# Cached keys rearranged in DRAM ahead of the attention stage, bias rows of the samples built once, and the T sums on VectorE

## The chip, the cores and the metric

The kernel runs on one core of one Trainium2 chip. A core has five engines with an instruction queue each: TensorE (PE in the profile, its weight loads PEld), VectorE (DVE), ScalarE (ACT), GpSimd (POOL) and SyncE (SP). An engine works through its queue in order; an instruction that waits for a semaphore holds up all that is queued behind it. SyncE computes nothing here: its queue only issues transfers, and GpSimd and ScalarE issue some too. All transfers of the core share 16 DMA engines. The metric is the device time of one execution in microseconds (us).

## The reference

One step of an encoder trunk for two groups with the same weights: 512 new rows of one stream (the prompt) and 16 new rows for each of 8 running streams (the samples), 640 rows of 2048 values in all. A shared projection w_in makes queries, keys, values and gates for 16 heads: 6 stick-breaking heads, 6 chunk-band softmax heads with a learned bias by distance, and 4 heads into memory tokens. The samples also attend to cached keys and values.

```python
(sq, sk, sv, sg, bq, bk, bv, bg, mq, mg, gsb, gbd, gmm) = in_projection(x, g_pre, w_in)
k_all = concatenate([cache_sb_k, sk2], axis=1)              # 8 x (512 + 16) x 6 x 128
o_sb2 = stick_breaking(sq2, k_all, v_all, q_pos_s, k_pos_sb)
o_bd2 = band_attention(bq2, kb, vb, q_pos_s, k_pos_bd, rel_bias)   # softmax(q k^T / sqrt(128) + bias)
o_mm2 = memory_attention(mq2, cache_mem_k, cache_mem_v)     # 8 x 256 x 4 x 128
merged = sigmoid(gsb)*((o_sb*silu(sg)) @ w_up_sb) + sigmoid(gbd)*(...) + sigmoid(gmm)*(...)
y = x + rms_norm(merged @ w_out, g_post)
```

Everything is float32. The keys, values and outputs of the new rows are returned as well.

## The kernel before, in words

**Precision.** Each float32 operand is split into a high part (ScalarE copies and rounds) and a low part (VectorE subtracts); the helper `split` does both, at L101 and L102, for every operand in the program. A product is three matmuls: high by high, high by low, low by high. So each 128x512 piece of weight costs one ScalarE and one VectorE instruction before TensorE can use it.

**Stages.** First the memory tokens are projected and the normed rows are transposed into x (tiles xh, xl, in four quarters b11, b12, b21, b22). Then four *gates*: column blocks of w_in, each 96 matmuls at L173. Beside them `sums` (L690 to L701) makes the operands T1 to T4 of a Strassen-type scheme out of the quarters of x: for each of four pieces k it adds high and low part of the four quarters (L695, tiles r1, r2, r3, r4; b11 and b12 on VectorE, b22 and b21 on GpSimd), stores r3, which is b12 again, to DRAM (L696), subtracts four times (L698, three on GpSimd and the last on VectorE) and splits the results (tiles th, tl). The tiles rs are taken from the three buffers of the tag ws.

**The pair stage.** 34 *pairs* of 128-column blocks of w_in follow (`block_pair`): `load_quads` (L716) loads four tiles of 512 KB on SP's queue, GpSimd forms the sums and differences s1 to s4 of weight quarters (L730, L777; the same tag ws), and TensorE does seven products of 24 matmuls each (L737). The first 12 pairs make the queries, keys, values and gates of the band heads, which go to DRAM (raw_d); the others make merge gates (sig_d). The weight tiles have three buffers in each of two tags (wr and wr2), so loads run about a pair ahead, each waiting until the split of an earlier tile has released its buffer.

**The attention stage.** 16 heads in a fixed order by a list of numbers. For each head the remaining projections run (L173, weights by L128), and three generators are interleaved: the prompt's attention, the samples' scores and the samples' outputs. For the scores `sample_score` brings in the cached keys of two streams at a time: `load_k` (L495) issues four transfers, one for each 32 columns of the head, which take runs of 32 values (128 bytes) and set them in the tile kc so that a blockwise transpose of VectorE (L506, tile kt) gives keys by columns. kc has two buffers. The cached values come by L546 (tile vc, eight transfers a head). For a band head the bias rows of the samples are loaded in eight transfers of 16 partitions (L594, tile st1) and eight of 16x8x16 values (L598, st3); GpSimd masks st3 twice and reorders it to st2 (L603, L605). natk (L629) is a store: new keys go out in four transfers of 128-byte runs.

**The end.** The up-projections follow (L173 again, results merged at L861 to L864), then the output projection (L158 to L160) and the norm.

The program is written with a tile framework. A scheduler that simulates a timeline sets the final order of every engine's queue, so instructions of neighbouring heads and pairs are mixed; `issue_after(x)` makes an instruction stand behind x in that order. These are the lines for the keys and for T:

```python
SP.dma_start(t[32 * a:32 * a + 32],                       # L495, for a in 0..3
             ck[b:b + 2, :, 32 * a:32 * a + 32].rearrange("b (c j) i -> j (b c) i", j=32))
DVE.transpose(kt, kc[:, h * nc_:(h + 1) * nc_])           # L506
for eng, t, q in ((DVE, r1, b11), (POOL, r2, b22), (DVE, r3, b12), (POOL, r4, b21)): ...      # L695
for eng, t, x, y in ((POOL, r1, r3, r1), (POOL, r3, r2, r3), (POOL, r2, r2, r1), (DVE, r4, r4, r2)): ...  # L698
```

Of the kernel before, what the change touches and what calls it, by code (L numbers as in the profile page):

```python
# [8 lines left out]
F32 = mybir.dt.float32  # L9
F32R = mybir.dt.float32r  # L10
AF = mybir.ActivationFunctionType
ALU = mybir.AluOpType
# [4 lines left out]
P = 128  # L17
# [4 lines left out]
NB = 8  # L22
TS = 16
NT = TP + NB * TS
HF = NT // 2
PAST = 512
NMEM = 256
# [11 lines left out]

C_SB, C_BD, C_MM, C_GATE = 0, 3072, 6144, 7168  # L40
# [3 lines left out]
def stream_step_kernel(  # L44
# [29 lines left out]


# [5 lines left out]
    kv_d = dpool.tile([NMEM, 1024], F32, name="kv_d")  # L81
    osg_d = [dpool.tile([P, NT], F32, name=f"osg_d{i}") for i in range(16)]
# [4 lines left out]
    sig_d = [dpool.tile([P, NT], F32, name=f"sig_d{i}") for i in range(3 * KB)]  # L87

# [105 lines left out]
    with ExitStack() as m0:  # L194
# [45 lines left out]
        mtmp = pm.tile([P, P], F32, name="mtmp")  # L240
# [7 lines left out]
        POOL.tensor_scalar(nsb, msb, -1.0, 1.0, op0=ALU.mult, op1=ALU.add)  # L248

# [29 lines left out]
        def load_bias():  # L279
# [4 lines left out]
            POOL.dma_start(rext_d, rext)  # L284

# [48 lines left out]

    def ext_ap(h, off, dims):
        t = rext_d[h:h + 1, off:off + 1]
        return bass.AP(tensor=t.tensor, offset=t.offset, ap=dims)
# [147 lines left out]
    def sample_score(ck, qr, kr, kind, strips, left):  # L485

        nkb = ck.shape[1] // P
        nc_ = nkb * P
        new = kind != "mm"

        def load_k(b):

            t = pa.tile([P, 32, 32], F32, tag="kc", name="kc", bufs=B["kc"])[:, :2 * nc_ // 32]
            for a in range(4):
                SP.dma_start(t[32 * a:32 * a + 32],  # L495
                             ck[b:b + 2, :, 32 * a:32 * a + 32].rearrange("b (c j) i -> j (b c) i", j=32))
            return t.rearrange("p c i -> p (c i)")
# [85 lines left out]
    def causal_head(i):  # L583

        kind, h, c0 = ("sb", i, C_SB) if i < 6 else ("bd", i - 6, C_BD)
        ck, cv = ((cache_sb_k, cache_sb_v), (cache_band_k, cache_band_v))[i // 6]
        kp, vp, ks, vs = (tokens(t)[:, h] for t in ((sbk_p, sbv_p, sbk_s, sbv_s), (bdk_p, bdv_p, bdk_s, bdv_s))[i // 6])
        strip, strips = None, None
        if kind == "bd":
            strip = pa.tile([P, 512], F32, tag="strip", name="strip")  # L590
            SP.dma_start(strip, ext_ap(h, 0, [[1, P], [1, 512]]))
            st1 = pa.tile([P, 512], F32, tag="st1", name="st1")
            for bb in range(NB):
                SP.dma_start(st1[bb * TS:(bb + 1) * TS], ext_ap(h, 128, [[1, TS], [1, 512]]))  # L594
            st2 = pa.tile([P, P], F32, tag="st2", name="st2")
            st3 = pa.tile([P, P], F32, tag="st3", name="st3")
            for bb in range(NB):
                SP.dma_start(st3[bb * TS:(bb + 1) * TS], ext_ap(h, 112, [[1, TS], [0, NB], [1, TS]]))  # L598

            with tc.issue_after(last_on(POOL)):  # L600
                POOL.memset(strip[0:64, 0:64], NEG)
                for base, cm, step in ((TS - P, 1, TS), (P - 1, -1, -TS)):
                    POOL.affine_select(st3, st3, pattern=[[step, NB], [0, TS]], compare_op=ALU.is_ge,  # L603
                                       fill=NEG, base=base, channel_multiplier=cm)
# [373 lines left out]
```

## Time and profile before

| what | value |
|---|---|
| time, median of 3 runs | 2138.67 us (2134.91 to 2139.42) |
| the profiled execution, its time | 2134.09 us |
| its span in the trace | 2132.4 us |
| PE, PEld, DVE, ACT, POOL busy in the span | 97%, 91%, 53%, 38%, 28% |
| DMA queue of SP | 541310 packets, 265.51 MB, 46.4% of 16 engines' span |
| packets under 512 bytes | 277841 of 554394 |
| chain of waits by engine | PE 85%, issue 4%, DMA 4%, DVE 2%, POOL 2%, SP's queue 2% |

A busy share is a mean over stages. The stages follow each other in time: memory and norm until 78 us, gates until about 134, pairs until 981, attention until about 1733, then up-projection and output. PE's busy time hides one thing: the granted clock, which falls to half for some microseconds after TensorE has stood still, is a column of its own. "Waits" name for each idle time of an engine what ended it; the chain goes back from the last instruction through what released each step.

### The profile page before, as it was taken

How to read it: one execution, taken by the hardware profiler on the slowest of the kernel's cores; microseconds unless marked ns; L12 is line 12 of the kernel's file. 1: busy time of each engine (PE TensorE's matmuls, PEld its weight loads, DVE VectorE, ACT ScalarE, POOL GpSimd, SP SyncE). 2: the span in 40 equal slices, each digit the busy share in tenths (PEclk: the TensorE clock that was granted, in tenths of full speed). 3: DMA queues.
4: the chain of work that ended last, by engine and by line, in shares of the span. 5: the costliest groups of instructions: out<-in, count | busy, mean ns of one | idle time of the engine just before them, and what ended most of it. 6: DMA issues, size and time to landing. Idle time of an engine off the chain costs nothing.

```text
span 2132.4 us, 36113 instructions
## 1 busy us (share of the span) xinstructions
PE 2058.5 (97%) x13997; PEld 1945.9 (91%) x13997; DVE 1128.3 (53%) x1788; ACT 815.5 (38%) x1567; POOL 599.0 (28%) x557
## 2 busy tenths in 40 slices
PE   8999999999999999999998899999997899999998
PEld 6999999999999999999988798989996799998886
DVE  6895555565555555554445546554445554542234
ACT  7534444444444444443223334333333232332221
POOL 0385455664444444440010101110100004330000
PEclk9999999999999999999999999999999899999999
DMA  7633333333333333335858669875665966542225
GB/s 248 198 105 115 129 121 105 105 104 115 123 127 104 105 104 112 124 122 119 196 125 206 143 152 201 208 157 137 151 160 134 249 182 193 173 133 79 79 76 221
DMA packets 554394, 305.86 MB, mean 143 GB/s; under 512 B 277841, under 2 KB 513377, under 8 KB 552685
## 3 DMA queue, kind: packets, MB, share of 16 engines
q1 hardware_dynamic: 541310, 265.51, 46.4%
q0 software_dynamic: 6000, 22.30, 2.8%
q10 hardware_dynamic: 6912, 15.73, 1.9%
q8 instruction: 110, 1.80, 0.4%
q14 instruction: 62, 0.51, 0.1%
HBM read 258.11 MB, written 45.37 MB: 142 GB/s over the span
## 4 chain that ended last, share of the span: by engine, by line
PE 85%; issue 4%; DMA 4%; DVE 2%; POOL 2%; SPq 2%; ACT 1%; DVEq 0%; POOLq 0%; ACTq 0%
PE q L737 39%; PE acc L173 26%; PE ya L160 3%; PE ya L158 3%; PE ya L159 3%; PE s L510 1%; POOL merged L864 1%; PE o L569 1%; SPq L495 1%; DMA kc<-in_cache_sb_k_dram 1%; PE tp L438 1%; PE acc L158 1%; PE acc L160 1%; DVE wl L102 1%; PE acc L159 1%
## 5 line engine op out<-in xcount | busy, mean ns | idle before, releaser
L102 DVE TENSOR_TENSOR wl<-wr,wh 128x512 fp32r<-128x512 f32 (+1 forms) x524 | 396.4, 761 | 395.1 <-ACT wh L101 385.7
L101 ACT CAST wh<-wr 128x512 fp32r<-128x512 f32 (+1 forms) x524 | 316.4, 608 | 651.5 <-PE acc L173 250.7
L102 DVE TENSOR_TENSOR wl<-ws,wh 128x512 fp32r<-128x512 f32 x272 | 244.1, 900 | 221.4 <-ACT wh L101 220.1
L737 PE MATMUL q<-xh,wl 128*128 128x320 f32 x1088 | 338.1, 311 | 4.2 <-DVE wl L102 4.2
L737 PE MATMUL q<-xh,wh 128*128 128x320 f32 x1088 | 337.7, 310 | 0.0
L737 PE MATMUL q<-xl,wh 128*128 128x320 f32 x1088 | 337.6, 310 | 0.0
L101 ACT CAST wh<-ws 128x512 fp32r<-128x512 f32 x272 | 169.1, 622 | 270.5 <-PE q L737 231.4
L173 PE MATMUL acc<-xh,wl 128*128 128x320 f32 x1152 | 271.5, 313 | 0.0
L173 PE MATMUL acc<-xh,wh 128*128 128x320 f32 x1152 | 269.2, 313 | 0.0
L173 PE MATMUL acc<-xl,wh 128*128 128x320 f32 x1152 | 269.1, 312 | 0.0
L737 PE MATMUL q<-th,wl 128*128 128x320 f32 x816 | 252.2, 309 | 0.0
L737 PE MATMUL q<-th,wh 128*128 128x320 f32 x816 | 252.1, 309 | 0.0
L737 PE MATMUL q<-tl,wh 128*128 128x320 f32 x816 | 252.1, 309 | 0.0
L737 PEld LDWEIGHTS q<-xh,wl 128*128 128x128 f32 x1088 | 206.0, 189 | 4.8 <-DVE wl L102 4.8
L737 PEld LDWEIGHTS q<-xh,wh 128*128 128x128 f32 x1088 | 205.8, 189 | 0.1
L737 PEld LDWEIGHTS q<-xl,wh 128*128 128x128 f32 x1088 | 205.8, 189 | 0.0
L173 PEld LDWEIGHTS acc<-xh,wh 128*128 128x128 f32 x1152 | 194.4, 189 | 10.4 <-issue 7.5
L173 PEld LDWEIGHTS acc<-xl,wh 128*128 128x128 f32 x1152 | 194.9, 190 | 6.3 <-issue 6.3
L173 PEld LDWEIGHTS acc<-xh,wl 128*128 128x128 f32 x1152 | 195.2, 190 | 2.8 <-issue 2.3
L730 POOL TENSOR_TENSOR ws<-wr 128x512 f32<-128x512 f32 x102 | 148.6, 1470 | 80.0 <-DVE wl L102 78.0
L777 POOL TENSOR_TENSOR ws<-wr,ws 128x512 f32<-128x512 f32 x68 | 89.7, 1319 | 232.9 <-DVE wl L102 232.9
L737 PEld LDWEIGHTS q<-th,wl 128*128 128x128 f32 x816 | 153.2, 188 | 0.2 <-DVE wl L102 0.2
(237 smaller groups left out, 3362.6 us busy)
## 6 DMA issues: line engine op xcount, KB each, us to landing
wr<-in_w_in_dram SPq DMA_DIRECT2D x208, 512.0 KB, 4.7
wr<-in_w_out_dram SPq DMA_DIRECT2D x32, 512.0 KB, 3.8
sig_d<-sig ACTq DMA_DIRECT2D x48, 320.0 KB, 4.3
sig<-sig_d SPq DMA_DIRECT2D x48, 320.0 KB, 3.6
kc<-in_cache_sb_k_dram SPq DMA_DIRECT2D x96, 128.0 KB, 3.6
vc<-in_cache_sb_v_dram SPq DMA_DIRECT2D x48, 256.0 KB, 5.8
kc<-in_cache_band_k_dram SPq DMA_DIRECT2D x96, 128.0 KB, 3.7
vc<-in_cache_band_v_dram SPq DMA_DIRECT2D x48, 256.0 KB, 5.4
```

Of the source, the lines that this page charges most:

```text
L101: ACT.copy(hi, src)
L102: DVE.tensor_tensor(lo, src, hi.bitcast(F32), op=ALU.subtract)
L158: PE.matmul(out, ah, bh, start=start, stop=False)
L159: PE.matmul(out, ah, bl, start=False, stop=False)
L160: PE.matmul(out, al, bh, start=False, stop=stop)
L173: PE.matmul(acc[:, s, :HF], a[:, k], b[s], start=first and f, stop=last and l)
L438: PE.transpose(tp[:, kb * P:(kb + 1) * P], b[:, kb * P:(kb + 1) * P], ident)
L495: SP.dma_start(t[32 * a:32 * a + 32], ck[b:b + 2, :, 32 * a:32 * a + 32].rearrange("b (c j) i -> j (b c) i", j=32))
L510: return PE.matmul(s[32 * j:32 * j + 32, :nc_], qm[:, j, par * 32:par * 32 + 32], kts[j], start=par == 0, stop=par == 1, tile_position=(0, ...
L730: eng.tensor_tensor(o, a[c], b[c], op=op)
L737: PE.matmul(bank_, a[:, k], b[:, k], start=first and k == 0 and n == 0, stop=k == KH - 1 and n == 2, skip_group_check=not first)
L777: POOL.tensor_tensor(b, a, b, op=ALU.subtract)
```

## The change

1. `cut_keys` (new) copies the cached keys of every head from the input to new DRAM tensors keys_d, DRAM to DRAM, in the layout that kc wants. It uses the same four transfers for two streams as `load_k` did, on SP's queue. 64 such cuts of four transfers (12 heads at 128 KB a transfer, 4 memory heads at 64 KB) are handed out two after each pair from the second one on, in the heads' order (the list ORDER), behind the last SP instruction of that pair.
2. `load_k` becomes one transfer for two streams: 128 partitions of two runs of 2048 bytes (1024 for memory heads) from keys_d.
3. The bias rows of the samples are built once, after rext_d, by six DRAM to DRAM transfers of GpSimd into st_d (128 rows of 528 values for each band head). A band head then takes one load instead of sixteen. The mask (tile mbd) is made once at the start; a head's st2 is one GpSimd addition.
4. In `sums` GpSimd keeps only r4 = b21; VectorE does the other three sums and all four differences.

```diff
+ORDER = (0, 6, 1, 7, 12, 2, 8, 3, 9, 13, 4, 5, 14, 15, 10, 11)
+
 C_SB, C_BD, C_MM, C_GATE = 0, 3072, 6144, 7168
 
 
...
+    mbd = const.tile([P, P], F32, name="mbd")
+
 
     xq = [[None, None], [None, None]]
     for i, j in ((0, 0), (0, 1), (1, 0), (1, 1)):
...
+    st_d = [dpool.tile([P, TS + 512], F32, name=f"st_d{h}") for h in range(6)]
+
+    keys_d = [dpool.tile([P, NB, (NMEM if i >= 12 else PAST)], F32, name=f"keys_d{i}") for i in range(16)]
     osg_d = [dpool.tile([P, NT], F32, name=f"osg_d{i}") for i in range(16)]
...
+    def ext_ap(h, off, dims):
+        t = rext_d[h:h + 1, off:off + 1]
+        return bass.AP(tensor=t.tensor, offset=t.offset, ap=dims)
 
...
-        mtmp = pm.tile([P, P], F32, name="mtmp")
+        mtmp = pm.tile([P, P], F32, tag="junk", name="mtmp")
...
+        ntmp = pm.tile([P, P], F32, tag="junk", name="ntmp")
+        POOL.memset(ntmp, 0.0)
+        for base, cm, step in ((TS - P, 1, TS), (P - 1, -1, -TS)):
+            POOL.affine_select(ntmp, ntmp, pattern=[[step, NB], [0, TS]], compare_op=ALU.is_ge,
+                               fill=NEG, base=base, channel_multiplier=cm)
+        POOL.tensor_copy(mbd.rearrange("p (a j i) -> p a j i", a=2, i=TS),
+                         ntmp.rearrange("p (j a i) -> p a j i", a=2, i=TS))
...
             POOL.dma_start(rext_d, rext)
+
+            for h in range(6):
+                POOL.dma_start(st_d[h].rearrange("(b t) n -> b t n", t=TS),
+                               ext_ap(h, 112, [[0, NB], [1, TS], [1, TS + 512]]))
...
-        nkb = ck.shape[1] // P
-        nc_ = nkb * P
+        nc_ = ck.shape[2]
         new = kind != "mm"
 
         def load_k(b):
 
             t = pa.tile([P, 32, 32], F32, tag="kc", name="kc", bufs=B["kc"])[:, :2 * nc_ // 32]
-            for a in range(4):
-                SP.dma_start(t[32 * a:32 * a + 32],
-                             ck[b:b + 2, :, 32 * a:32 * a + 32].rearrange("b (c j) i -> j (b c) i", j=32))
-            return t.rearrange("p c i -> p (c i)")
+            t = t.rearrange("p c i -> p (c i)")
+            SP.dma_start(t.rearrange("p (b n) -> p b n", b=2), ck[:, b:b + 2])
+            return t
 
...
-        ck, cv = ((cache_sb_k, cache_sb_v), (cache_band_k, cache_band_v))[i // 6]
+        cv = (cache_sb_v, cache_band_v)[i // 6]
         kp, vp, ks, vs = (tokens(t)[:, h] for t in ((sbk_p, sbv_p, sbk_s, sbv_s), (bdk_p, bdv_p, bdk_s, bdv_s))[i // 6])
         strip, strips = None, None
         if kind == "bd":
             strip = pa.tile([P, 512], F32, tag="strip", name="strip")
             SP.dma_start(strip, ext_ap(h, 0, [[1, P], [1, 512]]))
-            st1 = pa.tile([P, 512], F32, tag="st1", name="st1")
-            for bb in range(NB):
-                SP.dma_start(st1[bb * TS:(bb + 1) * TS], ext_ap(h, 128, [[1, TS], [1, 512]]))
+            st = pa.tile([P, TS + 512], F32, tag="st1", name="st1")
+            SP.dma_start(st, st_d[h])
             st2 = pa.tile([P, P], F32, tag="st2", name="st2")
-            st3 = pa.tile([P, P], F32, tag="st3", name="st3")
-            for bb in range(NB):
-                SP.dma_start(st3[bb * TS:(bb + 1) * TS], ext_ap(h, 112, [[1, TS], [0, NB], [1, TS]]))
 
             with tc.issue_after(last_on(POOL)):
                 POOL.memset(strip[0:64, 0:64], NEG)
-                for base, cm, step in ((TS - P, 1, TS), (P - 1, -1, -TS)):
-                    POOL.affine_select(st3, st3, pattern=[[step, NB], [0, TS]], compare_op=ALU.is_ge,
-                                       fill=NEG, base=base, channel_multiplier=cm)
-                POOL.tensor_copy(st2.rearrange("p (a j i) -> p a j i", a=2, i=TS),
-                                 st3.rearrange("p (j a i) -> p a j i", a=2, i=TS))
-            strips = (st1, st2)
+                POOL.tensor_tensor(st2.rearrange("p (g i) -> p g i", i=TS), mbd.rearrange("p (g i) -> p g i", i=TS),
+                                   st[:, None, 0:TS].to_broadcast([P, NB, TS]), op=ALU.add)
+            strips = (st[:, TS:], st2)
...
-                sample_score(ck[0, :, :, h], qr, kn, kind, strips, left),
+                sample_score(keys_d[i], qr, kn, kind, strips, left),
                 sample_out(cv[0, :, :, h], vn, sg, left, i))
 
     def mem_head(h):
...
-                sample_score(cache_mem_k[0, :, :, h], None, None, "mm", None, left),
+                sample_score(keys_d[12 + h], None, None, "mm", None, left),
...
-        for eng, t, q in ((DVE, r1, b11), (POOL, r2, b22), (DVE, r3, b12), (POOL, r4, b21)):
+        for eng, t, q in ((POOL, r4, b21), (DVE, r1, b11), (DVE, r3, b12), (DVE, r2, b22)):
             eng.tensor_tensor(t, q[0][:, ks].bitcast(F32), q[1][:, ks].bitcast(F32), op=ALU.add)
         POOL.dma_start(b12_d[:, ks], r3)
-        for eng, t, x, y in ((POOL, r1, r3, r1), (POOL, r3, r2, r3), (POOL, r2, r2, r1), (DVE, r4, r4, r2)):
-            eng.tensor_tensor(t, x, y, op=ALU.subtract)
+        for t, x, y in ((r1, r3, r1), (r3, r2, r3), (r2, r2, r1), (r4, r4, r2)):
+            DVE.tensor_tensor(t, x, y, op=ALU.subtract)
...
+    def cut_keys(i, b0, n):
+
+        src, h = ((cache_sb_k, i), (cache_band_k, i - 6), (cache_mem_k, i - 12))[min(i // 6, 2)]
+        for a in range(4):
+            SP.dma_start(keys_d[i][32 * a:32 * a + 32, b0:b0 + n].rearrange("j b (c i) -> j (b c) i", i=32),
+                         src[0, b0:b0 + n, :, h, 32 * a:32 * a + 32].rearrange("b (c j) i -> j (b c) i", j=32))
+
     pairs = [(C_BD + 768 * n + h * P, put_raw(n, h)) for n in range(4) for h in range(0, 6, 2)]
     pairs += [(C_GATE + i * P, put_gate(i)) for i in range(FIRST, 3 * KB, 2)]
+    cuts = [(i, b, 2) for i in ORDER for b in range(0, NB, 2)]
     for n, (col, put) in enumerate(pairs):
         block_pair(col, put, n == 0, n == len(pairs) - 1)
+
+        with tc.issue_after(last_on(SP)):
+            for _ in range(2):
+                if n and cuts:
+                    cut_keys(*cuts.pop(0))
...
-        for h in (0, 6, 1, 7, 12, 2, 8, 3, 9, 13, 4, 5, 14, 15, 10, 11):
+        for h in ORDER:
```

The scheduler sets the order anew. Three places matter below. First SP's queue in the pair stage (wr: weight tiles of the pairs; keys_d: the rearranged keys). Before, the four loads of a pair, which those of the next pair follow directly:

```order
L716 DMA wr<-in_w_in_dram 128x4x256
L716 DMA wr_2517<-in_w_in_dram 128x4x256
L716 DMA wr<-in_w_in_dram 128x4x256
L716 DMA wr_2521<-in_w_in_dram 128x4x256
```

and in the changed kernel:

```order
L727 DMA wr_2049<-in_w_in_dram 128x4x256
L727 DMA wr<-in_w_in_dram 128x4x256
L727 DMA wr_2053<-in_w_in_dram 128x4x256
L824 DMA keys_d_90<-in_cache_sb_k_dram 32x32x32 x8
L727 DMA wr<-in_w_in_dram 128x4x256
```

Eight transfers of 128 KB now stand between the four weight loads of one pair and those of the next.

Second, SP's queue in the attention stage while the second stick-breaking head is prepared (kc: cached keys; st: bias rows; natk: store of new keys; vc: cached values; l, sg: tiles of the band heads made in the pair stage; wr: weights of the projection). Before:

```order
L128 DMA wr<-in_w_in_dram 128x8x128 x3
L495 DMA kc<-in_cache_sb_k_dram 32x32x32 x8
L598 DMA st_12058<-rext_d 16x8x16 x6
L495 DMA kc<-in_cache_sb_k_dram 32x32x32 x4
L594 DMA st_12048<-rext_d 16x512
L495 DMA kc<-in_cache_sb_k_dram 32x32x32 x2
L629 DMA out_dram<-natk 32x16x32 x4
...
L594 DMA st_12048<-rext_d 16x512 x4
L598 DMA st_12058<-rext_d 16x8x16 x2
L353 DMA l_12092<-raw_d_1_101 128x640
L128 DMA wr<-in_w_in_dram 128x8x128 x2
```

and in the changed kernel:

```order
L141 DMA wr<-in_w_in_dram 128x8x128 x4
L514 DMA kc<-keys_d_91 128x1024 x2
L141 DMA wr<-in_w_in_dram 128x8x128
L514 DMA kc<-keys_d_91 128x1024
L611 DMA st_12284<-st_d_85 128x528
L514 DMA kc<-keys_d_91 128x1024
L640 DMA out_dram<-natk 32x16x32 x4
L373 DMA l_12306<-raw_d_1_124 128x640
L564 DMA vc<-in_cache_band_v_dram 128x4x128 x8
L141 DMA wr<-in_w_in_dram 128x8x128
```

From one weight load to the next over the whole row of keys, bias rows and values there were 45 transfers; now there are two stretches of 2 and 16.

Third, VectorE beside the gates, one piece of `sums` (rs, r, rx: the sums and differences; wl: low parts of the gates' weights; tl: low parts of T). Before:

```order
L698 TENSOR_TENSOR rs<-rs 128x640
L695 TENSOR_TENSOR rs<-xh_73,xl_74 128x640
L102 TENSOR_TENSOR tl_912<-rs,th_911 128x640
L102 TENSOR_TENSOR wl<-wr,wh 128x512
L102 TENSOR_TENSOR tl_919<-rs,th_918 128x640
```

and in the changed kernel:

```order
L706 TENSOR_TENSOR rs<-xh_74,xl_75 128x640
L706 TENSOR_TENSOR rs<-xh_80,xl_81 128x640
L709 TENSOR_TENSOR rs<-r_1223,rs 128x640
L115 TENSOR_TENSOR wl<-wr,wh 128x512
L709 TENSOR_TENSOR r_1223<-rs,r_1223 128x640
L115 TENSOR_TENSOR tl_952<-rs,th_951 128x640
L709 TENSOR_TENSOR rs<-rs 128x640
```

VectorE no longer meets results of GpSimd inside a piece except r4, and has four more instructions in each of the four pieces.

More of the change, by code (lines that the diff above doesn't have):

```diff
@@ L333, in masked @@
         return bass.AP(tensor=ap.tensor, offset=ap.offset, ap=[part, [64, n], [48, 2], [1, TS]])
-    def ext_ap(h, off, dims):
-        t = rext_d[h:h + 1, off:off + 1]
-        return bass.AP(tensor=t.tensor, offset=t.offset, ap=dims)
     def ins_of(x):
```

## The prediction

> **What bounds the kernel now.** I read the table of stages first: the stretch, then busy time (and instructions) of PE, PEld, DVE, ACT and POOL, the granted clock, the share of the DMA engines, GB/s.
>
> ```profile
> 0.00:78.00 78.00, 69.83 (x313) 52.19 (x314) 57.42 (x125) 55.97 (x104) 4.40 (x15) 0.96 0.69 237
> 78.00:130.00 52.00, 52.00 (x356) 51.96 (x356) 42.63 (x36) 21.71 (x34) 36.10 (x24) 1.00 0.45 146
> 130.00:300.00 170.00, 165.83 (x1104) 165.06 (x1104) 106.52 (x118) 67.17 (x120) 96.49 (x72) 0.97 0.36 118
> 300.00:981.00 681.00, 681.00 (x4644) 680.78 (x4643) 375.84 (x474) 309.15 (x552) 332.07 (x238) 1.00 0.34 111
> 981.00:1733.00 752.00, 699.62 (x5398) 644.92 (x5398) 385.25 (x770) 257.31 (x560) 65.64 (x173) 0.96 0.74 173
> ```
>
> TensorE never pauses in the pair stage, and its clock is full. The DMA engines idle there for two thirds of the time. In the attention stage it is the other way round: the DMA share is 0.74, TensorE stands still for 752 - 699.6 = 52 us, and the clock is 0.96. So whatever goes from the second stage to the first moves from a place where it may be waited for to one with room.
>
> Second, who ends TensorE's waits. The first four rows are of the attention stage, the last is the only wait at the pair stage's start (total, times, longest).
>
> ```profile
> PE tp L438 <- DVE b L463: 16.1, 4, 8.6
> PE acc L173 <- ACT wh L101: 11.6, 1, 11.6
> PE o L159 <- DVE wtl L102: 8.8, 2, 4.6
> PE o L158 <- ACT wth L101: 3.9, 6, 1.5
> PE q L737 <- DVE wl L102: 4.2, 2, 3.0
> ```
>
> These name VectorE and ScalarE, but the chain of waits tells what those two had waited for (start, duration, what):
>
> ```profile
> 1112.29 5.73 DMA vc<-in_cache_band_v_dram
> ...
> 1118.09 5.28 DMA wr<-in_w_in_dram
> ...
> 1192.23 3.97 DMA kc<-in_cache_mem_k_dram
> ...
> 1208.39 6.99 DMA kc<-in_cache_sb_k_dram
> ...
> 1420.65 6.77 DMA kc<-in_cache_sb_k_dram
> ...
> 1642.13 6.51 DMA st<-rext_d
> 1648.65 10.38 DMA wr<-in_w_up_sb_dram
> ...
> 1695.27 3.32 DMA kc<-in_cache_band_k_dram
> ```
>
> The waits of the first three rows, seven in all and 36.5 of the 52 us, lie but for about 1 us right behind these pieces: around 1118, 1196, 1213, 1425, 1648 and 1695. Each is a transfer late on SP's queue: VectorE stands at a key transpose or ScalarE at a weight tile, with the work that TensorE needs queued behind.
>
> Third, how SP's queue is filled (start, time from the first to the last issue, count), and the transfers by line:
>
> ```profile
> 983.57 8.37 SPq L495 DMA_DIRECT2D kc<-in_cache_sb_k_dram  x6
> 1043.69 3.05 SPq L629 DMA_DIRECT2D out_dram<-natk  x4
> 1047.31 7.62 SPq L495 DMA_DIRECT2D kc<-in_cache_band_k_dram  x9
> 1640.35 4.10 SPq L598 DMA_DIRECT2D st<-rext_d  x8
> kc<-in_cache_sb_k_dram SPq DMA_DIRECT2D x96, 128.0 KB, 3.6
> kc<-in_cache_band_k_dram SPq DMA_DIRECT2D x96, 128.0 KB, 3.7
> kc<-in_cache_mem_k_dram SPq DMA_DIRECT2D x64, 64.0 KB, 2.7
> st<-rext_d SPq DMA_DIRECT2D x48, 32.0 KB, 2.3
> ```
>
> A key transfer of 128 KB holds the queue for 0.85 to 1.4 us, a bias transfer for 0.5.
>
> **Price of a 128-byte run.** Three stretches of one kind of traffic each: stores of natk alone, key loads alone, weight rows of 512 bytes alone.
>
> ```profile
> 1045.50:1047.50 2.00, 2.00 (x8) 0.55 (x6) 0.01 (x1) 0.98 (x2) 0.29 (x1) 1.00 0.75 122
> 1050.00:1055.50 5.50, 5.50 (x41) 5.49 (x40) 4.11 (x7) 0.62 (x1) 0.00 (x0) 1.00 1.02 161
> 1207.00:1208.00 1.00, 1.00 (x9) 1.00 (x8) 0.20 (x1) 0.71 (x3) 0.00 (x0) 1.00 1.06 321
> ```
>
> Runs of 128 bytes move at 161/1.02 = 158 GB/s of full DMA time when they are read from DRAM, and at 122/0.75 = 163 when they are written to it. Longer rows move at 321/1.06 = 303.
>
> **The change, part by part.**
>
> *Cuts in the pair stage.* A pair lasts 168 of these matmuls:
>
> ```profile
> 144.40 836.44 PE q L737 x5686
> SPq L716 <- DVE wl L102: 747.3, 131, 20.0
> ```
>
> 836.44/5686 = 0.147 us, times 168 = 24.7 us. Its own traffic takes 0.34 x 24.7 = 8.4 us of the DMA engines, so 16.3 are free. Two cuts move 8 x 128 KB = 1.05 MB. No transfer from DRAM to DRAM in short runs exists before. Bounds: the price of the read alone, 1.05 MB/158 = 6.6 us, and read and write one after the other, 13.1. I take 8, near the lower row, since read and write were priced alike and can overlap. All three fit into 16.3. On SP's queue the eight issues take 8 x 0.85 to 1.4 = 7 to 11 us a pair, and SP waits 747/34 = 22 us a pair for a free weight tile. Behind the cuts stand the next pair's weight loads, and behind those GpSimd's combinations; a load is late only if the cuts last longer than SP's wait. Cost: 0 at either bound, because TensorE's matmuls cover it. Without that cover (16.3 us exceeded) every excess us counts once a pair.
>
> *Keys and bias rows in the attention stage.* The 256 key transfers become 64 of 2048-byte runs (1024 for memory heads), the 96 bias transfers become six. Key bytes: 192 x 131 KB + 64 x 66 KB = 29.4 MB. They took 29.4/158 = 186 us of the DMA engines and should take 29.4/303 = 97 at most: the stage's 0.74 x 752 = 556 us falls to about 465. SP issues 282 transfers fewer; at 0.5 to 1.4 us this is some 200 us of a queue that is hardly ever free.
>
> What can come back at most is the 52 us of standstill plus what the half clock cost on busy time. A clock of 0.96 over 752 us is 30 us; part of it fell on idle time, and I leave 22 (an estimate). Ceiling 74. Of the 36.5 us that chain to SP's queue I expect four fifths to go, 29: with the keys' and bias rows' issues gone, the weights and values behind them are the only ones left to be late. The other 15.5 end on softmax and sigmoid steps or follow on those stalls; a quarter goes, 4. That is 33 of 52, and of the clock the same part, 14. Sum 47 us. What is late next is the value loads (eight issues a head stay) and the head's own chain of scores, softmax and transposes, above all around 1615 to 1660, where few projection matmuls are left to fill. Bounds: 16 (the bias rows and a third of the stalls) and 70.
>
> *Bias rows made early.* GpSimd's queue around them before (start, duration, in brackets the idle time before it):
>
> ```profile
> 25.39 0.72 POOL L284 DMA_DIRECT2D rext_d<-rext  x1 [22.31 <-DVE rs L140]
> 60.15 0.79 POOL L315 DMA_DIRECT2D out_dram<-kv  x1 [34.04 <-ACT kv L314]
> ```
>
> The six transfers go into the 34 us of idle time, behind a wait for rext_d to land. They write 1.6 MB while the DMA engines are busy to 0.69 (first row of the stages): 1.6/237 is 7 us of that traffic, over some 35 us. 0, at most 3 us. The mask is four short GpSimd instructions in the idle time before: 0. The keys' new wait, on the cuts, is over long before the first head.
>
> *T sums.* Rows of GpSimd and VectorE (busy, mean ns), then three single VectorE instructions: the first sum, and two low parts of the same 128x512 shape, one alone and one beside GpSimd:
>
> ```profile
> L695 POOL TENSOR_TENSOR rs<-xh,xl 128x640 f32<-128x640 f32 x8 | 15.4, 1937 | 2.9 <-DVE tl L102 2.9
> L698 DVE TENSOR_TENSOR rs<-rs 128x640 f32<-128x640 f32 x4 | 3.3, 818 | 2.9 <-POOL rs L698 2.9
> L102 DVE TENSOR_TENSOR tl<-rs,th 128x640 fp32r<-128x640 f32 x12 | 15.8, 1332 | 0.7 <-ACT th L101 0.6
> 86.26 0.82 DVE L695 TENSOR_TENSOR rs<-xh,xl 128x640 f32<-128x640 f32 x1
> 96.73 0.68 DVE L102 TENSOR_TENSOR wl<-wr,wh 128x512 fp32r<-128x512 f32 x1
> 137.83 1.75 DVE L102 TENSOR_TENSOR wl<-wr,wh 128x512 fp32r<-128x512 f32 x1
> ```
>
> GpSimd loses 16 instructions of 1.9 us, VectorE gains 16 of 0.82. The 0.82 holds because VectorE's instructions are slow only beside GpSimd's (0.68 against 1.75). VectorE then has 28 sums at 0.82, 12 tl and 4 xl at 0.82 and 16 wl at 0.68: 47 us, from about 86 to 133. The four gates give 4 x 96 x 0.147 = 56 us from 78, to 134. So T is ready when the gates end, and the 4.2 us of waits before the first pair go, with the half clock behind them (0.03 x 170 = 5.1 us). At most 9; I take 8. Below: -3, if GpSimd's first combinations overlap the last sums and slow them.
>
> **Sum.** 8 + 0 + 47 = 55 us. The profiled execution took 2134.09 (span 2132.4 and 1.7 around it), so 2079 by it; the median of the runs, 2138.67, lies 4.6 higher and gives 2084. The time to be compared is a median, so I lean to the second: 2083.
>
> **Rivals.** *Short writes to DRAM cost a second access* (slower). If a run of 128 bytes into DRAM first had to be read back, a cut would take three times the read price: 19.7 us a pair, 3.4 more than the free 16.3. On the 24 pairs with cuts of causal heads (the eight with memory heads carry half) weight loads fall behind by 24 x 3.4 = 82 us; less the 55 gained this is 2138.7 + 27 = 2166. It decides from 16.3/6.6 = 2.5 times the read price on. Against it: natk writes the same runs to DRAM at 163 GB/s, no dearer than reads. For it: no row shows DRAM on both sides. The Trainium skill has such a rule (DMA: Bandwidth & Descriptors, Specifications: below 512 bytes the engine does a read-modify-write); natk's row does not bear it out.
>
> *The stalls only move.* If the heads' own chains set the gaps and the late keys merely lay upon them, the attention stage gives the lower bound of 16, and the time is 2138.7 - 24 = 2115. For it: ACT and DVE rows make up a third of the waits, and the scheduler's order is new everywhere. Against it: the six long stalls end on transfers.
>
> *The change does nothing that counts.* Values, weights and stores alone keep the queue full, and keys wait behind them as now: only T, 2131, or nothing. For it: 465 us of DMA time stay in the stage. Against it: 282 issues fewer.
>
> *All of it goes.* 9 + 70: 2060.
>
> **How the numbers follow.** Forecast 0.60 (2062 to 2103), stalls only move 0.16 (2103 to 2125), nothing that counts 0.07 (2125 to 2143), all of it 0.06, slower 0.11. This kernel's measurement tells 0.2%, about 4 us, from no change. Faster: 0.60 + 0.16 + 0.06 + half of 0.07 and a little = 0.86; same 0.03; slower 0.11. The range 2058 to 2116 leaves out the slower case, the weak end and about 0.02 below. The likeliest case's own range is 2062 to 2103.
>
> **What would show it.** Right: in the pair stage PE without waits, the DMA share up from 0.34 to 0.55 to 0.7, and SP's wait at the weight loads about 10 us a pair shorter; in the attention stage the share down towards 0.65, PE idle under 25 us, the clock at 0.98 or more, and no chain piece on kc above 3 us; no wait of the first pair's matmuls on wl. Wrong: matmuls of the pairs waiting on wl with the chain on wr or on GpSimd's combinations (the cuts are too dear), or idle in the attention stage as before with ACT and DVE at the chain's end.

## The result and the profile after

The changed kernel takes 2088.39 us (median of 4 runs, 2088.03 to 2090.27), the kernel before on the same chip 2137.10 (4 runs, 2134.91 to 2139.42). The ratio is 0.9774, with a 95% interval from 0.9757 to 0.9791: faster by 48.7 us. The forecast was 2083, with a range from 2058 to 2116. One correction to the description of the change: two streams' keys lie side by side in keys_d, so a partition's row in a key load is one run of 4096 bytes, not two of 2048 (2048 for memory heads).

The table of stages, cut this time where the chain of waits shows a stage's first matmuls to begin: start, gates, pairs, attention, end. The columns are the stretch, its length, then busy time (instructions) of PE, PEld, DVE, ACT and POOL, the granted clock, the DMA share, GB/s. Before:

```profile
0.00:78.20 78.20, 70.03 (x315) 52.34 (x316) 57.61 (x125) 55.97 (x104) 4.40 (x15) 0.96 0.69 236
78.20:144.40 66.20, 62.03 (x412) 61.26 (x410) 56.78 (x45) 26.04 (x41) 47.44 (x30) 0.96 0.45 144
144.40:980.80 836.40, 836.40 (x5687) 836.18 (x5688) 468.02 (x582) 371.80 (x665) 417.22 (x303) 1.00 0.35 112
980.80:1826.50 845.70, 792.91 (x6094) 737.52 (x6092) 432.34 (x844) 283.13 (x606) 97.22 (x192) 0.97 0.72 173
1826.50:2132.40 305.90, 297.16 (x1495) 258.54 (x1495) 113.58 (x194) 78.59 (x153) 32.67 (x18) 0.99 0.37 122
```

After:

```profile
0.00:80.30 80.30, 69.60 (x314) 51.83 (x315) 57.55 (x125) 56.25 (x104) 9.17 (x25) 0.98 0.75 251
80.30:136.70 56.40, 56.40 (x387) 56.40 (x386) 46.99 (x61) 25.06 (x39) 18.84 (x13) 1.00 0.53 165
136.70:974.60 837.90, 837.90 (x5713) 837.68 (x5712) 451.36 (x582) 373.31 (x667) 418.84 (x304) 1.00 0.57 147
974.60:1779.00 804.40, 783.77 (x6094) 730.23 (x6092) 434.99 (x844) 283.73 (x606) 90.91 (x180) 0.99 0.62 182
1779.00:2086.30 307.30, 297.42 (x1495) 258.55 (x1495) 113.49 (x194) 78.62 (x153) 32.39 (x18) 0.99 0.37 122
```

The span fell by 46.1 us: start +2.1, gates and pairs together 902.6 to 894.3 = -8.3, attention 845.7 to 804.4 = -41.3, end +1.4. (Gates and pairs have to be added: before, 26 of the first pair's matmuls lie ahead of 144.40.) In the attention stage TensorE's standstill, length less busy time, fell from 52.8 to 20.6 us, and its busy time, which holds the half clock, by 9.1.

The waits after: first TensorE's longest, then SP's queue (total, times, longest).

```profile
PE tp L458 <- DVE b L483: 7.3, 5, 3.2
PE o L171 <- ACT wth L114: 2.7, 3, 1.5
...
SPq L727 <- DVE wl L115: 438.1, 131, 12.2
SPq L514 <- DVE kt L524: 66.6, 43, 5.8
```

The matmuls of the first pair no longer wait on wl; and of the prediction's rows those on wh (11.6 us), wtl (8.8) and wl (4.2) have no successor above 2 us; the row on b, 16.1 us before, still has 7.3. SP waits at the pairs' weight loads 438 us instead of 747, 9.1 us a pair less. But at the key loads (L514) it now waits for a free key buffer, 66.6 us in all; the same wait took 34.7 before. The chain of waits of the changed kernel, its pieces for gates and pairs, then the transfers above 3 us that it holds between 975 and 1700 us, with the piece ahead of one of them:

```profile
80.34 56.32 PE acc L186 x384
136.66 837.98 PE q L748 x5712
...
1171.64 6.49 DMA kc<-keys_d
...
1380.20 1.27 DVE kt L524 x2
1381.49 3.52 DMA kc<-keys_d
1389.48 5.70 DMA kc<-keys_d
1592.57 7.27 DMA or<-osg_d
```

The chain now runs through TensorE from the gates' first matmul to the pairs' last without a gap. The prediction showed eight late transfers in this stage, four of them key loads; counted as here (above 3 us, 975 to 1700 us), the chain before held eleven, five of them key loads. Now there are four: three key loads, all for memory heads (their transposes are 256 wide), and the load of a head's output. Each of the three key loads is issued as a transpose (L524) ends that had held its buffer, as in the two lines at 1380 and 1381 us.

### The profile page after: what moved, and what is told of

The parts are those of the page before. It is cut to its first block, busy times and chain, and to the rows that moved or that the text cites. A ratio compares the mean times of both kernels' runs of the same rounds, so it can differ in the third digit from the quotient of the medians.

```text
span 2086.3 us, 35971 instructions
## 1 busy us (share of the span) xinstructions
PE 2045.1 (98%) x13997; PEld 1934.7 (93%) x13997; DVE 1104.4 (53%) x1804; ACT 817.0 (39%) x1567; POOL 570.1 (27%) x539
## 4 chain that ended last, share of the span: by engine, by line
PE 91%; DMA 2%; issue 2%; DVE 2%; POOL 1%; ACT 1%; SPq 0%; DVEq 0%; POOLq 0%; ACTq 0%
PE q L748 40%; PE acc L186 32%; PE ya L171 4%; PE ya L172 3%; PE ya L173 3%; PE s L528 2%; POOL merged L888 1%; PE o L587 1%; DMA kc<-keys_d 1%; DMA wr<-in_w_mem_kv_dram 1%; PE tp L458 1%; PE o L171 1%; DMA or<-osg_d 0%; PE o L172 0%; PE o L173 0%
## 5 line engine op out<-in xcount | busy, mean ns | idle before, releaser
L115 DVE TENSOR_TENSOR wl<-wr,wh 128x512 fp32r<-128x512 f32 (+1 forms) x524 | 383.0, 734 | 384.0 <-ACT wh L114 373.3
L115 DVE TENSOR_TENSOR wl<-ws,wh 128x512 fp32r<-128x512 f32 x272 | 231.3, 852 | 232.4 <-ACT wh L114 231.8
L748 PEld LDWEIGHTS q<-tl,wh 128*128 128x128 f32 x816 | 153.2, 188 | 0.0
```

The costliest lines, as they stand in the source:

```text
L115: DVE.tensor_tensor(lo, src, hi.bitcast(F32), op=ALU.subtract)
L748: PE.matmul(bank_, a[:, k], b[:, k], start=first and k == 0 and n == 0, stop=k == KH - 1 and n == 2, skip_group_check=not first)
```

## The experiments

Each was timed beside the kernel before on the same chip, whose median differed by up to 4 us from one set of runs to the next; so ratios are compared.

### One part at a time

Four kernels make one part of the change alone: only `sums`, only the bias rows and the mask, only the keys, and the cuts without a reader:

```diff
 # cuts_unread, this place against the change: keys_d is written in the pair stage,
 # load_k, the bias rows and the T sums stay as before
-                sample_score(keys_d[i], qr, kn, kind, strips, left),
+                sample_score(ck[0, :, :, h], qr, kn, kind, strips, left),
```

> Only the T sums go to VectorE; keys and bias rows stay as before. My theory: the weights of the pairs' T are ready when the gates end, so the stretch from the gates' first matmul to the pairs' first matmul shrinks by 8 to 10 us and nothing else moves: 2127 to 2129 us. Rival: the whole program gains only where the stalls of the attention stage end, and time won earlier is lost again in them: 2135 to 2139, no change.

> Only the bias rows are made once (six transfers at the start, one load a head) and the mask once; keys and T sums as before. My theory: the 96 issues of 0.5 us are few, the stall around 1645 us in which ScalarE waits for a weight tile behind the bias loads (11.6 us) goes, and 2 us are lost at the start: 2125 to 2135. Rival: the bias loads are what holds the queue before the heads' keys, and half of the attention stage's 41 us comes from here: 2115 or less.

> Only the keys go through the DRAM tensor in block order (cuts in the pair stage, one load per two blocks); bias rows and T sums as before. My theory: most of the attention stage's gain is the keys': 2098 to 2108, the pair stage as long as before. Rival: stalls only move, and without the fewer bias issues the keys give about a third of it: 2118 to 2127.

> The cuts are made in the pair stage, but nobody reads them: the heads load their keys as before, bias rows and T sums as before. It prices the cuts by themselves. My theory: the pair stage hides them whole, 2137 plus or minus 3, DMA share of the pair stage 0.56, the attention stage as before. Rival: they cost something (a late weight load, a later end of the pairs, contention with the heads' first loads) that the keys' gain hides in the whole change: 2145 or more.

| kernel | median, us | ratio to before (95%) | gain at 2140.6 |
|---|---|---|---|
| T sums alone | 2132.46 | 0.9963 (0.9950 to 0.9975) | 7.9 us |
| bias rows alone | 2105.76 | 0.9841 (0.9825 to 0.9857) | 34.0 us |
| keys alone | 2117.74 | 0.9891 (0.9878 to 0.9905) | 23.3 us |
| cuts that nobody reads | 2139.76 | 1.0007 (0.9995 to 1.0020) | none |

The kernel before took 2140.57 in this set. My theory held for the cuts: they cost nothing, within 0.2%. For the T sums the gain came out as forecast (7.9 us against 8 to 10); the time did not (2127 to 2129 us), because the kernel before took 2140.57 us in this set and 2137.10 in the one I started from. The theory was wrong on who carries the attention stage. The bias rows, 2 MB in 96 transfers, gain more than the 29.4 MB of keys in 256; for both the rival came closer: the bias rows' time lies in its range (2115 or less), that of the keys within 1 us of its (2118 to 2127). The attention stage of T sums, bias rows and keys alone, with the same columns as above:

```profile
975.90:1827.20 851.30, 796.05 (x6093) 739.36 (x6092) 432.01 (x844) 282.89 (x606) 97.81 (x192) 0.96 0.71 172
981.90:1803.70 821.80, 789.09 (x6094) 734.63 (x6093) 430.44 (x844) 282.46 (x606) 91.64 (x180) 0.98 0.74 178
982.80:1810.90 828.10, 790.20 (x6094) 733.91 (x6092) 432.63 (x844) 283.87 (x606) 98.93 (x192) 0.98 0.61 177
```

The bias rows leave the DMA share about where it was (0.74, 0.72 before) and still take standstill from 52.8 to 32.7 us. The keys take 0.11 off the share and leave 37.9. So the 20 us of standstill that go with the bias rows were not owed to the volume on the DMA engines; for the keys, volume and number of issues fall together, and these two rows cannot tell them apart. Which waits went is seen at ScalarE, where weight tiles are split, and at VectorE, where keys are transposed (total, times, longest, in the attention stage). Four kernels in this order: before, bias rows alone, keys alone, after.

```profile
ACT wh L101 <- DMA wr<-in_w_in_dram: 29.7, 4, 14.3
ACT wh L101 <- DMA wr<-in_w_up_sb_dram: 21.1, 5, 15.6
...
DVE kt L506 <- DMA kc<-in_cache_sb_k_dram: 18.7, 8, 8.9
DVE kt L506 <- DMA kc<-in_cache_band_k_dram: 11.6, 8, 2.7
...
DVE kt L506 <- DMA kc<-in_cache_mem_k_dram: 7.8, 4, 4.4
```

```profile
ACT wh L113 <- DMA wr<-in_w_up_sb_dram: 15.3, 5, 5.5
ACT wh L113 <- DMA wr<-in_w_in_dram: 7.3, 1, 7.3
...
DVE kt L525 <- DMA kc<-in_cache_sb_k_dram: 21.7, 6, 8.4
DVE kt L525 <- DMA kc<-in_cache_band_k_dram: 19.5, 10, 3.5
DVE kt L525 <- DMA kc<-in_cache_mem_k_dram: 5.7, 3, 2.7
```

```profile
ACT wh L104 <- DMA wr<-in_w_in_dram: 15.7, 2, 11.3
ACT wh L104 <- DMA wr<-in_w_up_sb_dram: 13.7, 2, 9.3
...
DVE kt L507 <- DMA kc<-keys_d: 31.2, 9, 10.6
```

```profile
ACT wh L114 <- DMA wr<-in_w_up_sb_dram: 0.5, 1, 0.5
...
DVE kt L524 <- DMA kc<-keys_d: 20.1, 11, 4.9
```

ScalarE waited 51 us for weights before, 23 with the bias rows made early, 29 with the keys cut early, and under 1 us with both. So either part shortens the waits for weights. VectorE's waits for keys were 38.1 us before; the keys alone shorten them by only 7, and with the bias rows alone they are longer, 46.9, though TensorE stands still 20 us less.

A fifth kernel leaves out only the keys:

> The change without its keys: bias rows made once and T sums on VectorE, key loads as before. Alone, the bias rows gained 34 us, the keys 23, the T sums 8: together 65, and the whole change 48. Theory (keys and bias rows remove the same late weight loads): T and bias add up, 2140 - 42 = 2098, and the keys are worth only some 7 to 9 us on top: 2094 to 2101. Rival (the T sums' gain is what gets lost in the whole, the keys keep their 23): 2106 to 2114.

It took 2103.73 us, ratio 0.9831 (0.9810 to 0.9851) against 0.9774 of the whole: on top of the rest the keys are worth 0.57%, 12 us, with an uncertainty of about 6. It fell between both numbers. By times the three parts alone add up to 65 us and the whole gains 48, so part of the keys' and the bias rows' gain would be one and the same. By the attention stage's lengths, one profiled execution each, there is no overlap: 23.9 for the bias rows and 17.6 for the keys make 41.5, the whole 41.3. I cannot decide between the two: the runs of before spread over 10 us and its profiled execution lies at their low end, while that of the bias rows (2111.38) is the slowest of its four. That the bias rows alone bring more than the keys alone holds by both.

The sums of waits above say what a part moved, not what it is worth. With only the keys left out, the waits are 30.2 us for weights and 57.0 for keys, in all as long as before (87 and 89), and still TensorE stands still for 32.0 us and not 52.8.

### Issues or short rows

Does a transfer cost its issue on SP's queue, or the drain of its short rows? Two kernels keep the rows long and bring back the number of issues:

```diff
 # bias_in_16: the bias rows alone, and in them
-            SP.dma_start(st, st_d[h])
+            for bb in range(0, P, 8):
+                SP.dma_start(st[bb:bb + 8], st_d[h][bb:bb + 8])
 # keys_bias_split: the same in the whole change, and each key load in four
-            SP.dma_start(t.rearrange("p (b n) -> p b n", b=2), ck[:, b:b + 2])
+            for a in range(0, P, 32):
+                SP.dma_start(t[a:a + 32].rearrange("p (b n) -> p b n", b=2), ck[a:a + 32, b:b + 2])
```

> bias_alone, but each head's prepared bias rows are loaded by 16 transfers of 8 partitions instead of one: as many issues on SP's queue as in the kernel before, the rows still long and the mask still made once. Issues theory: the 96 issues of 0.4 to 0.5 us ahead of the weight loads are the price, so the gain of 34 us goes back for the most part: 2128 to 2140. Rival, rows theory: the short rows of the old transfers (64 bytes, landing after 4.5 us) and GpSimd's mask made them dear, and 16 long ones cost little: 2104 to 2114.

> The whole change, with the bias rows of a head in 16 transfers and every key load in four of 32 partitions: SP issues as many transfers for the heads as before, but all of them move long rows. Issues theory (each issue costs the same): only the T sums' gain stays, 2125 to 2135. Rows theory (an issue is dear because a transfer of 128-byte rows holds the queue 0.85 to 1.4 us, and one of long rows 0.4): 96 x 0.4 us for the bias rows and 192 x 0.4 us more for the keys, and half of the attention stage's gain stays, 2102 to 2115. A third outcome, 2086 to 2094, would mean that neither issues nor bytes on SP's queue are the cause, but where the transfers stand in its order.

bias_in_16 took 2119.98 us, ratio 0.9904 (0.9884 to 0.9923): of the 34.0 us, 13.5 go back with 90 more issues and 20.5 stay. The time lies between the two ranges, so neither theory holds alone. keys_bias_split took 2112.94, ratio 0.9868 (0.9842 to 0.9895): 20 us of 48 go back with 282 issues, and 28 stay, 8 of them the T sums', as the rows theory had it (2102 to 2115). Their attention stages:

```profile
982.30:1811.40 829.10, 790.25 (x6094) 732.09 (x6092) 432.06 (x844) 283.10 (x606) 91.59 (x180) 0.97 0.72 176
977.10:1802.90 825.80, 789.02 (x6093) 730.76 (x6091) 432.00 (x844) 282.94 (x606) 91.82 (x180) 0.98 0.64 177
```

In bias_in_16 ScalarE waits for weights for less than with the bias rows alone (5.7 us against 22.6), and VectorE for its keys as long (47.1 against 46.9). The first row is TensorE's longest:

```profile
PE tp L457 <- DVE b L482: 14.4, 4, 10.2
...
ACT wh L113 <- DMA wr<-in_w_up_sb_dram: 4.8, 3, 2.6
ACT wh L113 <- DMA wr<-in_w_in_dram: 0.9, 1, 0.9
DVE kt L525 <- DMA kc<-in_cache_band_k_dram: 21.3, 7, 6.4
DVE kt L525 <- DMA kc<-in_cache_sb_k_dram: 15.9, 6, 6.8
DVE kt L525 <- DMA kc<-in_cache_mem_k_dram: 9.9, 5, 4.3
```

The one stall of 10.2 us ends at 1674 us behind a key transpose that waited 6.4 us for its load. On SP's queue that load stands behind 16 bias transfers (6.0 us), eight value loads (7.5) and four stores (3.8). So the issues cost time, but which load is late for them differs from kernel to kernel: before, the longest stall was for weights, here it is for keys. The scheduler orders each queue anew. What stays of the bias rows' 34 us can be the short rows (the old 8 KB transfers took 4.5 us to land at the median), GpSimd's masking of every head's rows, or the changed order of the queue. These three were not taken apart, and that stays open.

### What the pair stage can hide

The whole change with each cut made three times, and the same with four blocks to a transfer, so that half as many issues carry the same bytes:

```diff
+            for dst in (keys_d, *spare_d):
-            SP.dma_start(keys_d[i][32 * a:32 * a + 32, b0:b0 + n].rearrange("j b (c i) -> j (b c) i", i=32),
+                SP.dma_start(dst[i][32 * a:32 * a + 32, b0:b0 + n].rearrange("j b (c i) -> j (b c) i", i=32),
...
 # cuts_three_times_big
-    cuts = [(i, b, 2) for i in ORDER for b in range(0, NB, 2)]
+    cuts = [(i, b, 4) for i in ORDER for b in range(0, NB, 4)]
```

> The whole change with each cut made three times (twice into DRAM that nobody reads): it measures what the pair stage can hide. Bytes theory: a pair's cuts take 5.4 us of the DMA engines in the changed kernel (share 0.34 to 0.56), three times that is 16.2 of 16.3 free: 2088 to 2100 and a share near 1.0. Queue theory: a pair's eight issues took 9.1 us of SP's 22 us of waiting, 24 take 27, so SP falls 5 us a pair behind on some 31 pairs: 2180 to 2250, with the pairs' matmuls waiting on wl. If a short write into DRAM cost a second access (my slower rival, 19.7 us of DMA time a cut pair), three of them would be 59 us a pair against 16 free: over 3000.

> cuts_three_times with four blocks to a transfer: the same bytes and rows for each pair, in 12 transfers of 256 KB instead of 24 of 128 KB. Issues theory (each issue costs SP about 1 us, whatever it moves): 12 + 3 us of 24.7 a pair, hidden again: 2088 to 2105. Rows theory (the queue takes issues only as fast as the rows of 128 bytes drain, so an issue of twice the size takes twice as long): as cuts_three_times, 2240 to 2270.

They took 2255.86 us (ratio 1.0540, 1.0519 to 1.0561) and 2217.54 (1.0368, 1.0344 to 1.0392). The pair stage of both, TensorE's longest wait with three cuts, then the cuts' issues by line (duration of an issue in ns: shortest, median, longest) in the changed kernel, with three cuts, and with three big ones:

```profile
139.40:1147.10 1007.70, 895.03 (x5713) 877.78 (x5713) 526.87 (x582) 365.12 (x667) 448.59 (x304) 0.94 0.84 181
135.40:1100.20 964.80, 877.97 (x5715) 867.71 (x5714) 499.20 (x582) 366.34 (x667) 436.50 (x304) 0.95 0.88 189
```

```profile
PE q L749 <- ACT wh L115: 70.9, 18, 18.2
```

```profile
L824 SPq DMA_DIRECT2D keys_d<-in_cache_sb_k_dram x96: 552/862/3553, 131.9 to 710.5; - x96
```

```profile
L826 SPq DMA_DIRECT2D spare_d<-in_cache_sb_k_dram x192: 561/963/3312, 135.3 to 871.6; - x192
```

```profile
L826 SPq DMA_DIRECT2D spare_d<-in_cache_sb_k_dram x96: 561/1913/7032, 131.3 to 831.8; - x96
```

With three cuts the bytes theory (2088 to 2100) fails; the queue theory (2180 to 2250) comes within 6 us, and the pairs' matmuls wait for weights as it said, though on wh more than on wl. Twice the rows in a transfer, twice the time of its issue (963 and 1913 ns, 136 and 137 GB/s), while the shortest issue stays at 561. So under load SP gives out a transfer about as fast as its rows drain, and of the theories on the big cuts the one on rows (2240 to 2270) comes closer than the one on issues (2088 to 2105). The 37 us less than with small transfers (1.0368 against 1.0540) show that the number counts too. The Trainium skill (Perfetto Trace Analysis, DMA Instruction — HWDGE) has an issue's profiled time end only after all its descriptors have been generated, and lets the engines start earlier when there are more than the buffer holds. That the median doubles with the rows agrees with it; that the issue waits for the rows to drain is read from the two medians.

The price of a cut follows from the DMA shares. DMA time of the pair stage is 0.35 x 836.4 = 293 us before, 0.57 x 837.9 = 478 after, 0.84 x 1007.7 = 846 with three cuts. The 29.4 MB cut once took 185 us, three times 553: 159 GB/s both times, to some 3% as the shares have two digits, the same as reading alone (158 GB/s in the prediction). The expectation's 5.4 us a pair was a mean that takes in pairs with half-size cuts or none; a pair with two whole cuts takes 1.05 MB at 159 GB/s, 6.6 us. Three times that is 19.8, more than the free 16.3.

### The stalls that are left

The keys on GpSimd's queue, the bias rows' six transfers later, and both:

```diff
-            SP.dma_start(t.rearrange("p (b n) -> p b n", b=2), ck[:, b:b + 2])
+            POOL.dma_start(t.rearrange("p (b n) -> p b n", b=2), ck[:, b:b + 2])
 # bias_later: the loop with st_d[h] stands after the memory stage
```

> The whole change, with the key loads of the attention stage issued from GpSimd's queue instead of SP's. In the changed kernel SP stands 66.6 us for a free key buffer and 20.3 us at the keys' transfers, with weights and values behind. My theory: the last long gaps (1180 to 1197, 1385 to 1404 us) end behind these waits, and some 10 us of them and of the clock go: 2074 to 2082. Rival: the keys wait for their two buffers, whichever queue issues them, and GpSimd's stores of the heads' outputs now stand behind them: 2086 to 2096.

> The whole change with the six transfers that write the prepared bias rows issued after the memory stage instead of in the middle of it. The gates began 2.1 us later after the change (80.3 against 78.2 us) and a weight load behind these transfers was late. Theory: they cost these 2 us: 2085.5 to 2087.5 by the level of 2088.4. Rival: the start differs by that much from kernel to kernel (81.6 and 81.0 us with the T sums or the keys alone, which have no such transfers), and nothing changes: within 1.5 of the whole change.

> bias_later with the key loads on GpSimd's queue as in keys_on_pool (which came out 0.2% below the whole change, within its interval). A candidate for a faster kernel. Theory: the two add up, 2081 to 2086. Rival: both are nothing, 2086 to 2090.

They took 2088.05, 2087.18 and 2086.92 us, ratios 0.9752 (0.9731 to 0.9773), 0.9757 (0.9737 to 0.9778) and 0.9758 (0.9737 to 0.9778). Against 0.9774 (0.9757 to 0.9791) none can be told from the whole change. With the keys on GpSimd's queue, SP's waits at them are gone, but its attention stage and its chain read

```profile
975.80:1780.40 804.60, 784.27 (x6095) 731.10 (x6093) 433.49 (x844) 284.02 (x606) 125.50 (x244) 0.99 0.62 182
```

```profile
1112.20 7.08 DMA kc<-keys_d
1318.40 7.01 DMA kc<-keys_d
```

as long as the whole change's 804.4, with key loads late at other places. Issuing them elsewhere does not make them earlier, as the rival had it: the loads wait for one of kc's two buffers. GpSimd's queue shows this wait:

```profile
POOL kc L514 <- DVE kt L524: 223.2, 43, 25.5
```

It is the transposes that free the buffers, and 43 of the 64 loads wait for them, as many as on SP's queue. No run has a third buffer, so what one would bring is not known. bias_later lies in both of its ranges, and the traces decide. The start is no matter of the six transfers either: the gates begin at 80.3 us with them in the middle of the memory stage and at 80.2 with them later, and at 81.6 and 81.0 in the kernels with T sums or keys alone, which have none; over all kernels here they begin between 78 and 83.

## Why the prediction was right, and where not

**T sums** (predicted 8, bounds -3 to 9): 8.3 us between the gates' first and the pairs' last matmul, 7.9 by the times of the kernel that does nothing else. Mechanism and size were right: T is ready when the gates end, and the stretch of the gates is now 56.4 us with TensorE always busy. VectorE is busy for 47.0 us of it, against 47 forecast. Of the 8.3 us, 4.2 are standstill and 4.1 busy time, which goes with a granted clock of 0.96 before and 1.00 now in the gates' stretch; the prediction had 4.2 and 5.1.

**Cuts** (predicted 0; 8 us of DMA time a pair, bounds 6.6 and 13.1): the cost is 0 within 0.2%, by the cuts that nobody reads. The price is the lower bound, 6.6, not the 8 that I took: the write adds nothing to the read that the shares could show. The slower rival falls with it. A second access at each write would have made three times the read price; three cuts in place of one show 159 GB/s each. The Trainium skill's rule that it leaned on (DMA: Bandwidth & Descriptors, Specifications) is not borne out for 128-byte runs in this kernel. The break-even at 2.5 times the read price was crossed but not located: three cuts exceed the free time by 3.5 us on each of 24 pairs, 84 us. They cost 127 to 170: the engines' share stays at 0.84 to 0.88 over the stage, and SP's queue, which I had priced at a fixed 0.85 to 1.4 us an issue, slows with the load. That price came from two bursts; over all key loads of the causal heads before, the median issue took 0.57 and 0.67 us (L495).

**Attention stage** (predicted 47: 33 of standstill and 14 of clock; bounds 16 and 70): 41.3 us, of which standstill 32.2 and busy time 9.1. The standstill was right, and by its terms: the three rows of waits, 36.5 us, are down to 7.3, so 29.2 went where 29 were forecast. The clock's term is 5 of the 6 us missing here: I started from 22 us of half clock on busy time, an estimate out of the mean clock of 0.96, and took two thirds; 9.1 came back with three fifths of the standstill gone. Whether that term was too large is not shown. The unchanged attention stage took 845.7 us in the profile of the kernel before, but 851.3 with the T sums alone and 855.6 with the cuts that nobody reads. Against these two the changed stage gains 46.9 and 51.2 us, of which 12.3 and 14.9 are busy time.

What the sum hid is who brings it. The prediction did not divide it; my expectations gave the keys, with 192 fewer issues and 89 us less DMA time, the larger part, and the bias rows little. Alone, the bias rows bring 34 us and the keys 23. That the keys are what is late I had read from the chain, where four of the eight pieces are key loads; but the piece that ended the longest stall, 11.6 us, was a weight load behind bias loads, and ScalarE's 50.8 us of waits for weights were more than VectorE's 38.1 for keys. The chain could not have settled it either: on SP's queue eight key issues stand right ahead of those bias loads (4.1 us at 1640.35, in the prediction) and hold it for longer.

```profile
1633.17 7.07 SPq L495 DMA_DIRECT2D kc<-in_cache_band_k_dram  x8
```

Only the kernels with one part each tell them apart.

**Keys no longer late** (no chain piece on kc above 3 us): wrong. Pieces of 6.5, 3.5 and 5.7 us remain. The forecast had the value loads late next, because it took SP's queue for all that holds the keys up; it is the keys again, whichever queue issues them. What holds them now is kc's two buffers: SP's wait for a free one grew from 34.7 to 66.6 us, a term that the prediction did not have.

**Bias rows made early** (0, at most 3): nothing that can be measured. **The rest**: DMA share of the pairs 0.57 (0.55 to 0.7), of the attention stage 0.62 (0.65), standstill 20.6 (under 25), clock 0.99 (0.98). Start and end came out 2.1 and 1.4 us longer; the prediction had put both at nothing. The start varies that much between the kernels here, so no part of the change explains it; why the end grew by 1.4 is not known.

Sum: 8.3 + 41.3 - 2.1 - 1.4 = 46.1 against 55. By medians the gain is 48.7, which is why the time, 2088, lies 5 and not 9 us above the forecast.

## What to carry to other kernels

When several kinds of transfers share one queue, the transfer that ends the chain does not tell which of those ahead of it is worth removing. Here 96 bias transfers of 2 MB in all were worth more alone than 256 key transfers of 29.4 MB, and this showed only when each part was made alone. Rearranging data from DRAM to DRAM cost nothing in a stage that TensorE bounds, as long as its bytes at the price of the read (6.6 us a pair) fitted into the free DMA time (16.3). One profiled execution is a rough measure of a stage: the unchanged attention stage differed by 10 us between three of them.

## What the runs showed of the hardware

The issues of the changed kernel's key loads (shortest, median, longest, ns):

```profile
L514 SPq DMA_DIRECT2D kc<-keys_d x64: 319/338/2321, 974.5 to 1635.3; - x64
```

Copies from DRAM to DRAM in runs of 128 bytes cost the DMA engines no more than reading such runs into SBUF: 159 GB/s of full DMA time once and three times over (to some 3%), against 158. An issue on SP's queue is not a fixed price: 0.34 us at the median for key loads of up to 512 KB in rows of 4096 and 2048 bytes, 0.86 for 128 KB in rows of 128 bytes, 0.96 when more of them are queued, 1.91 for twice the rows.
